# VectorE's order at three layer ends of a two-layer encoder: a norm pass, a low part and a weight split queued later

## The chip, the cores and the metric

The kernel runs on one core of one Trainium2 chip. The metric is the time on the device in microseconds (us) of one execution; a kernel's time is the median of its runs. Beside the timed runs there is one profiled execution, whose trace gives the start and duration of every instruction on the engines: PE (TensorE), DVE (VectorE), ACT (ScalarE), POOL (GpSimd) and SP (SyncE, which only issues transfers here).

## The reference

512 tokens of width 1024 go through two layers. Each layer has a token mixer and an MLP of width 4096, and each of these four is followed by a residual sum and a LayerNorm:

```python
def reference(x, ...):
    for i in range(DEPTH):                      # DEPTH = 2
        j = i // N_MIXERS
        if i % N_MIXERS == 0:
            m = _mixer_gdn(x, ...)              # gated delta rule, both directions, 8 heads of 128
        else:
            m = _mixer_gla(x, ...)              # gated linear attention, both directions, 4 heads
        x = _layernorm(DEEPNORM_ALPHA * x + m.astype(x.dtype), ln1_g[i], ln1_b[i])
        x = _layernorm(DEEPNORM_ALPHA * x + _sq_relu_mlp(x, mlp_w1[i], mlp_w2[i]).astype(x.dtype), ln2_g[i], ln2_b[i])
    return x
```

Both mixers end in a product of the mixed heads (512 x 1024) with `w_out` (1024 x 1024). The MLP is `relu(x w1)` squared, times `w2`. All is float32.

## The kernel before, in words

**Arithmetic.** Every large product is made of three matmuls on rounded halves: an operand is split into a high part, a cast on ScalarE, and a low part, a subtraction on VectorE (`split`, L96 and L101 for weights and hidden values). A product is high x high (L122), then the two mixed ones (L123, L124), made in `mm3`. Where a matmul is named `pj<-xth,wh`, `pj` is the PSUM bank it adds to, and `xth` / `xtl` are the high and low parts of the transposed activations, `wh` / `wl`, `ah` / `al`, `w2h` / `w2l` those of weight blocks or of other operands.

**Stages.** In the trace, the delta-rule mixer takes about the first 425 us, the first MLP runs from 425 to 762, the linear-attention mixer (`gla`) from 752 to 1004, the second MLP from 1004 to the end. The 512 tokens are four tiles of 128 (tile 0 to 3; `xt` 5559 to 5562 in the queues shown below). A layer's normed output is wanted transposed by the next layer's first products, which run in two halves of 256 tokens (tiles 0 and 1, then 2 and 3); the work of tiles 2 and 3 at a layer's end thus runs beside the first half of the next layer's products.

**A layer end** does for each tile:
- the last matmuls of the sublayer into PSUM, and the residual sum on VectorE (L332 at a mixer's end; L625, the line of `full`, at the MLP's, whose bank is `pX`); at the delta-rule mixer's end the residual is added on TensorE instead (`in_ps=True`);
- mean and variance. `layernorm` (the delta-rule mixer's end) uses VectorE's statistics, `norm_halves` (the others) adds up the mean on VectorE (L259), squares on ScalarE (L249, L250) and adds the variance (L264);
- a first norm pass of two halves, (z - mean) x gain (L236 or L263);
- the reciprocal root (`rsqrt`: L196 and L197 on ScalarE, then L198, L199, L200, L205 on VectorE, each of which needs the one before);
- a second pass of two halves, times that root, plus the bias (L241 or L270);
- `xpose`: two groups of four transposes on TensorE (L184) into a bank `tp`, a cast to `xth` on ScalarE (L187), a subtraction to `xtl` on VectorE (L188), for each group.

The `tp` banks are one at the delta-rule mixer's end and two in `gla`. After a mixer, VectorE adds high and low of the activations up again for a block scheme of the MLP (`x_blocks`, L420 and L426 to L429 into memory called `w2r`).

**Weights.** `wcols` loads a block of 128 columns (512 KB) into a staging buffer `wst` (three of them, by SyncE's queue, L50) and splits it. The first three blocks of the MLP's `w1` are loaded and split before its start (`take_ahead`); the fourth goes to memory called `ah` / `al`. SyncE's queue is in order: a load that waits for a free buffer holds those behind it, among them the loads of `w2` (`w2r`).

**The first work of `gla`** has a low-rank product `gps` (L147, L148) and, on ScalarE, the gate weights `w2r` (L847, L848 here), which take memory that the MLP's norm parameters `ln` had.

**What sets the order.** Each engine runs its own queue in order. The order of the queues is set when the program is built, by a scheduler that follows the place in the program: what is written first comes first unless it isn't ready in the scheduler's own reckoning. Two means bend this. `in_order(engine)` ties the instructions written inside it on an engine in the order of writing; TensorE's order is tied so in most stages. `issue_after(i)` keeps the instructions written inside it behind instruction `i` in the queue of `i`'s engine; it adds no wait on the chip. `normed` holds the ScalarE and VectorE instructions of the last norm's rsqrt and second pass (`normed[1]` is the latter), `last_hi` and `last_lo` those of the last `xpose`.

`out_last` makes the last matmuls of a mixer's output, the norm and `xpose`. `mlp`'s `last` does the same for the MLP's end and returns `norm`, which is called for tiles 2 and 3 behind it; after the first MLP, `xpose` for those tiles is called in `gla`, between the matmuls of its first products.

Of the kernel before, what the change touches and what calls it, by code (L numbers as in the profile page):

```python
# [17 lines left out]
P = 128  # L18
# [3 lines left out]
NT = S // P  # L22
# [6 lines left out]
class Ctx:  # L29
# [279 lines left out]
    def out_last(self, w, ks, lhs, z, tags, par, homes=None, xtags=("tp",), ahead=None, in_ps=True):  # L309

        nc = self.nc
        homes = iter(homes or ())
        ws = [{k: self.wrows(w, k * P, hf * 512, next(homes, None)) for k in ks[hf][::2]} for hf in range(2)]
        if ahead:
            ahead()
        if not in_ps:
            sums = [self.small.tile([P, 2], F32, name="lns", tag="lns") for t in range(NT)]
            stats = [[self.small.tile([P, 2], F32, name=f"lnv{q}", tag=f"lnv{q}") for q in range(2)] for t in range(NT)]  # L320
        pss = {}
        for t, hf in [(t, hf) for t in range(NT - 2) for hf in range(2)] + [(NT - 2, 0), (NT - 1, 0), (NT - 2, 1), (NT - 1, 1)]:
            sl = slice(t * P, (t + 1) * P)
            ps = pss[t, hf] = self.bank([P, 512], F32, name="ob", tag=tags[hf % len(tags)])
            if in_ps:
                nc.tensor.matmul(ps, self.ident, z[t][hf], start=True, stop=False)
            for i, k in enumerate(ks[hf]):
                ah, al = lhs(k, sl)
                wh, wl = ws[hf][k - i % 2]
                self.mm3(ps, ah, al, wh[:, i % 2, :], wl[:, i % 2, :], not in_ps and i == 0, i == len(ks[hf]) - 1)  # L330
            if not in_ps:
                nc.vector.scalar_tensor_tensor(z[t][hf], ps, 1.0, z[t][hf], ALU.mult, ALU.add, accum_out=sums[t][:, hf:hf + 1])  # L332
                self.half_stats(z[t][hf], sums[t][:, hf:hf + 1], stats[t][hf], ps)
            if hf:
                if in_ps:
                    self.layernorm([pss[t, 0], pss[t, 1]], self.xh(t), par)
                else:
                    self.norm_halves(z[t], par, sums[t], stats[t], (0, 1))
                if in_ps or t < NT - 2:
                    self.xpose(t, self.xt[t], xtags)  # L340
        if not in_ps:
            with self.tc.issue_after(self.normed[1].ins):
                self.xpose(NT - 2, self.xt[NT - 2], xtags)
            self.xpose(NT - 1, self.xt[NT - 1], xtags)


def mlp(c, w1, w2, g, b, out=None, extra=None):
# [8 lines left out]
    tc, nc = c.tc, c.nc  # L356
# [5 lines left out]
    with c.banks(pj=2, X=2, Y=2, Z=2), tc.tile_pool(name="mlp", bufs=2) as pool:  # L362
# [5 lines left out]
        def ring(name):  # L368
            return (pool, *RING[name])
# [36 lines left out]
        def new_h():  # L406
            return [pool.tile([P, HF, S], F32, name="h", tag="h", bufs=3) for _ in range(2)]
# [192 lines left out]
        def last(gi, h, a):  # L600
# [90 lines left out]
            for j in range(2):  # L691
# [1 line left out]
            return norm, second_normed  # L693

        h = new_h()
        specs = [(c.ahead[f] if f < len(c.ahead) else c.wcols(w1, f * P, pool=ring("ah") if f == 3 else None),
                  "pj", ("pj", "pj", "X", "X")[f]) for f in range(4)]
        for f, ps in enumerate(c.proj_halves(specs)):
            act(ps, h[0][:, f, :])
# [70 lines left out]
            h, a = nh, stream.a  # L770
        with c.in_order(mybir.EngineType.PE):
            norm, normed = last(G - 1, h, a)
        norm(2)
        norm(3)
        c.normed = normed

# [123 lines left out]
class GlaHead:  # L900
# [199 lines left out]
    def norm(self):  # L1100

        c, h = self.c, self.h
        V, A, T = c.nc.vector, c.nc.scalar, c.nc.tensor
        gcol = self.consts[-1]
        rs = c.small.tile([P, NT], F32, name="rs", tag="rs")
        c.rsqrt(rs, self.ss, NT, RMS_EPS)
        for n, o in self.ob.items():
            V.scalar_tensor_tensor(o, o, rs[:, n:n + 1], self.sr[:, n, :], ALU.mult, ALU.mult)
        for i in range(2):
            ps = c.bank([P, NT, P], F32, name="otp", tag="tp")  # L1110
            for n in range(NT):
                T.transpose(ps[:, n, :], self.ob[n][:, i * P:(i + 1) * P], c.ident)
            hi = self.oth[:, 2 * h + i, :].rearrange("p (n t) -> p n t", n=NT)
            lo = self.otl[:, 2 * h + i, :].rearrange("p (n t) -> p n t", n=NT)
            A.mul(hi, ps, gcol[:, i:i + 1])
            V.scalar_tensor_tensor(lo, ps, gcol[:, i:i + 1], hi.bitcast(F32), ALU.mult, ALU.subtract)
# [654 lines left out]
def body(tc, nc, a, out):  # L1771
    with contextlib.ExitStack() as es:
        def pool(name, bufs, **kw):
            return es.enter_context(tc.tile_pool(name=name, bufs=bufs, **kw))

        c = Ctx(tc, nc, (pool("const", 1), pool("big", 1), pool("wst", 3), pool("whl", 3), pool("small", 4)))
        x = a["x"][0]
        gdn(c, a["a_w_in"][0], a["a_conv"][0], a["a_alog"][0], a["a_dt_bias"][0], a["a_norm_g"][0],
            a["a_w_out"][0], a["ln1_g"][0], a["ln1_b"][0], x, a["mlp_w1"][0])
        with tc.tile_pool(name="gcst", bufs=1) as gp:  # L1780
            gc = []
            mlp(c, a["mlp_w1"][0], a["mlp_w2"][0], a["ln2_g"][0], a["ln2_b"][0],
                extra=lambda tmp: gc.append(GlaConst(c, gp, a["b_gate_b"][0], a["b_norm_g"][0], tmp)))
            gla(c, gc[0], a["b_w_in"][0], a["b_gate_w2"][0], a["b_w_out"][0], a["ln1_g"][1], a["ln1_b"][1], a["mlp_w1"][1])
        mlp(c, a["mlp_w1"][1], a["mlp_w2"][1], a["ln2_g"][1], a["ln2_b"][1], out=out[0])
# [18 lines left out]
```

## Time and profile before

| what | value |
|---|---|
| median of 3 runs | 1340.41 us (1339.39 to 1340.73) |
| profiled execution | 1341.23 us, of which the span from the first to the last instruction 1339.4 |
| mean granted TensorE clock | 0.996 |
| busy: PE / DVE / ACT / POOL | 1317.2 / 1099.9 / 800.5 / 123.3 us |
| read from HBM / written | 113.99 MB / 2.10 MB |

TensorE has work in nearly the whole span; the clock that it was granted is full but for the first and last slices. A row of the timeline has the start, the duration, the engine, the line, the operation, the tiles (out<-in), the shape and how many alike (x2) are put together, and in brackets for how long the engine stood idle before it and what it waited for. Small differences in idle time on TensorE show in the distance from one start to the next, too. Rows of "waits" give an engine, an operation and line, whom it waited for, the us in all, how often, and the longest.

### The profile page before, as it was taken

Reading aid. Unit: us, or ns where it says so; the run is one execution under the profiler, and the core shown is the slowest. Engines: PE = TensorE matmul, PEld = TensorE weight load, DVE = VectorE, ACT = ScalarE, POOL = GpSimd, SP = SyncE. Lnnn points to the kernel's source line nnn. Section 1 sums busy time; section 2 is a strip of 40 time slices with the busy share of each in tenths; the row PEclk is TensorE's granted clock in tenths of the full one; section 3 lists DMA queues with packets and bytes.
Section 4 is the critical chain, followed back from the end, with each engine's and each line's share of the span. In section 5 each row is a group of like instructions: output and inputs, shape, how many; then the busy total and the mean of one; then the engine's idle time right before and its main releaser. Section 6 shows DMA issues by size and latency. Waiting matters only on the chain.

```text
span 1339.4 us, 22232 instructions
## 1 busy us (share of the span) xinstructions
PE 1317.2 (98%) x8629; PEld 1124.4 (84%) x8629; DVE 1099.9 (82%) x1802; ACT 800.5 (60%) x1590; POOL 123.3 (9%) x177
## 2 busy tenths in 40 slices
PE   8999999999999999999999999999999999999996
PEld 8777878777777889999998888888889899999985
DVE  6797878788778878988988877967879678989888
ACT  4667657767643645666566754654456456565656
POOL 4000000000000910100102100000001001101011
PEclk9999999999999999999999999999999999999998
DMA  6221112112232674775748532221327475757556
GB/s 179 64 65 47 35 46 64 48 49 72 72 96 63 210 161 149 161 179 150 171 124 176 138 111 71 63 64 63 94 64 208 107 186 137 165 170 147 156 136 148
DMA packets 155660, 154.35 MB, mean 115 GB/s; under 512 B 7723, under 2 KB 122531, under 8 KB 155555
## 3 DMA queue, kind: packets, MB, share of 16 engines
q1 hardware_dynamic: 143779, 110.85, 27.8%
q0 software_dynamic: 11776, 42.08, 16.1%
q8 instruction: 68, 1.11, 0.3%
q14 instruction: 37, 0.30, 0.1%
HBM read 113.99 MB, written 2.10 MB: 87 GB/s over the span
## 4 chain that ended last, share of the span: by engine, by line
PE 86%; DVE 6%; ACT 6%; issue 1%; DMA 1%; DVEq 0%; POOL 0%; ACTq 0%; POOLq 0%
PE pX L123 3%; PE pX L122 3%; PE pX L124 3%; PE fx L124 3%; PE fx L123 3%; PE fx L122 3%; PE pjv L123 3%; PE m L1694 3%; PE pjv L122 3%; PE pjv L124 3%; PE pj L123 3%; PE pj L124 3%; PE pj L122 3%; PE fyz L124 2%; PE fyz L122 2%; PE fyz L123 2%
## 5 line engine op out<-in xcount | busy, mean ns | idle before, releaser
L101 DVE TENSOR_TENSOR wl<-wst,wh 128x1024 fp32r<-128x1024 f32 x148 | 182.3, 1232 | 49.1 <-ACT wh L96 47.8
L96 ACT CAST wh<-wst 128x1024 fp32r<-128x1024 f32 x150 | 157.7, 1051 | 101.1 <-PE fyz L123 30.1
L101 DVE TENSOR_TENSOR w2l<-w2r,w2h 128x1024 fp32r<-128x1024 f32 x92 | 112.7, 1225 | 27.2 <-ACT w2h L96 27.1
L96 ACT CAST w2h<-w2r 128x1024 fp32r<-128x1024 f32 x94 | 98.4, 1048 | 56.3 <-PE pX L124 24.8
L402 POOL DMA_DIRECT2D w2r<-w2r x56 | 48.4, 891 | 503.1 <-DVE w2l L101 290.1
L96 ACT CAST ah<-h 128x1024 fp32r<-128x1024 f32 x56 | 58.8, 1051 | 51.8 <-PE pZ L123 23.2
L451 DVE TENSOR_TENSOR wst<-wst 128x512 f32<-128x512 f32 x110 | 73.5, 688 | 0.2
L101 DVE TENSOR_TENSOR al<-h,ah 128x1024 fp32r<-128x1024 f32 x56 | 68.6, 1224 | 5.2 <-ACT ah L96 5.2
L123 PE MATMUL pX<-w2l,ah 128*128 128x512 f32 x168 | 66.1, 394 | 0.0
L122 PE MATMUL pX<-w2h,ah 128*128 128x512 f32 x168 | 66.0, 393 | 0.0
L124 PE MATMUL pX<-w2h,al 128*128 128x512 f32 x168 | 65.7, 391 | 0.0
L123 PE MATMUL pj<-xtl,wh 128*128 128x256 f32 (+1 forms) x192 | 64.6, 338 | 0.6 <-DVE xtl L188 0.6
L122 PE MATMUL pj<-xth,wh 128*128 128x256 f32 (+1 forms) x192 | 64.2, 338 | 0.3 <-ACT xth L187 0.2
L124 PE MATMUL pj<-xth,wl 128*128 128x256 f32 (+1 forms) x192 | 64.5, 337 | 0.0
L122 PE MATMUL pjv<-wh,xth 128*128 128x512 f32 x128 | 54.4, 425 | 0.0
L124 PE MATMUL pjv<-wh,xtl 128*128 128x512 f32 x128 | 50.2, 392 | 0.0
L123 PE MATMUL pjv<-wl,xth 128*128 128x512 f32 x128 | 50.0, 390 | 0.0
L124 PE MATMUL fx<-xh,wl 128*128 128x256 f32 x176 | 49.7, 283 | 0.0
L124 PE MATMUL fyz<-xh,wl 128*128 128x256 f32 x176 | 49.7, 282 | 0.0
L124 PE MATMUL fx<-xth,wl 128*128 128x256 f32 x176 | 49.7, 282 | 0.0
L123 PE MATMUL fx<-xtl,wh 128*128 128x256 f32 x176 | 49.7, 282 | 0.0
L122 PE MATMUL fyz<-xh,wh 128*128 128x256 f32 x176 | 49.7, 282 | 0.0
(528 smaller groups left out, 4319.1 us busy)
## 6 DMA issues: line engine op xcount, KB each, us to landing
wst<-in_mlp_w SPq DMA_DIRECT2D x68, 512.0 KB, 4.9
w2r<-in_mlp_w SPq DMA_DIRECT2D x60, 512.0 KB, 4.4
w2r<-w2r POOLq DMA_DIRECT2D x56, 512.0 KB, 5.6
wst<-in_a_w_in SPq DMA_DIRECT2D x32, 512.0 KB, 4.0
wst<-in_b_w_in SPq DMA_DIRECT2D x32, 256.0 KB, 3.0
wst<-in_a_w_out SPq DMA_DIRECT2D x8, 512.0 KB, 3.6
wst<-in_b_w_in SPq DMA_DIRECT2D x8, 512.0 KB, 4.2
wst<-in_b_w_out SPq DMA_DIRECT2D x8, 512.0 KB, 3.7
```

The costliest lines, as they stand in the source:

```text
L96: h = nc.scalar.copy(hi, src)
L101: self.halves = h, nc.vector.tensor_tensor(lo, src, hi.bitcast(F32), ALU.subtract)
L122: mm(ps, ah, bh, start=start, stop=False, **kw)
L123: mm(ps, ah, bl, start=False, stop=False, **kw)
L124: self.last_mm = mm(ps, al, bh, start=False, stop=stop, **kw)
L402: nc.gpsimd.dma_start(blocks[a + (q,)], blocks[b + (q,)], accum_op=ALU.add)
L451: plus = lambda a, b: V.tensor_tensor(a, a, b, ALU.add)
L1694: T.matmul(ps[:, d, :], *ops(d), start=True, stop=True)
```

## The change

Three edits, all on the order in which work is queued; no instruction is added or taken away.

1. `out_last`: the `xpose` calls of tiles 2 and 3 come behind the whole loop at the delta-rule mixer's end too (`in_ps=True`), with the lows of tile 2 behind tile 3's second norm pass. Before, this held for `gla`'s end alone.
2. `mlp`: in the second MLP (`out` is given) the split of the fourth weight block gets a place behind the last `xpose`'s high and low.
3. `mlp`: after the first MLP, `norm(2)` gets a place behind tile 1's second norm pass.

```diff
--- before.py
+++ after.py
@@ -336,12 +336,11 @@
                     self.layernorm([pss[t, 0], pss[t, 1]], self.xh(t), par)
                 else:
                     self.norm_halves(z[t], par, sums[t], stats[t], (0, 1))
-                if in_ps or t < NT - 2:
+                if t < NT - 2:
                     self.xpose(t, self.xt[t], xtags)
-        if not in_ps:
-            with self.tc.issue_after(self.normed[1].ins):
-                self.xpose(NT - 2, self.xt[NT - 2], xtags)
-            self.xpose(NT - 1, self.xt[NT - 1], xtags)
+        with self.tc.issue_after(self.normed[1].ins):
+            self.xpose(NT - 2, self.xt[NT - 2], xtags)
+        self.xpose(NT - 1, self.xt[NT - 1], xtags)
 
 
 def mlp(c, w1, w2, g, b, out=None, extra=None):
@@ -693,7 +692,8 @@
             return norm, second_normed
 
         h = new_h()
-        specs = [(c.ahead[f] if f < len(c.ahead) else c.wcols(w1, f * P, pool=ring("ah") if f == 3 else None),
+        specs = [(c.ahead[f] if f < len(c.ahead) else c.wcols(w1, f * P, pool=ring("ah") if f == 3 else None,
+                                                                 late=() if out is None else (c.last_hi, c.last_lo)),
                   "pj", ("pj", "pj", "X", "X")[f]) for f in range(4)]
         for f, ps in enumerate(c.proj_halves(specs)):
             act(ps, h[0][:, f, :])
@@ -770,7 +770,8 @@
             h, a = nh, stream.a
         with c.in_order(mybir.EngineType.PE):
             norm, normed = last(G - 1, h, a)
-        norm(2)
+        with contextlib.nullcontext() if out is not None else tc.issue_after(normed[1].ins):
+            norm(2)
         norm(3)
         c.normed = normed
```

From the first edit on, the new program's lines are one lower (L625 is L624, L420 is L419), and behind the third one higher (L847 is L848). How the queues stand:

VectorE at the end of the delta-rule mixer, before; `xt_5562` is tile 3, the L188 are lows of tiles 2 and 3, `al<-wst,ah` is the fourth weight block's low, and `w2r<-xth,xtl` the first sums of `x_blocks`:

```order
L205 TENSOR_TENSOR rstd<-rsy,rst 128x1
L241 SCALAR_TENSOR_TENSOR xt_5562<-xt_5562,rstd,lnp 128x512
L188 TENSOR_TENSOR xtl<-tp,xth 128x4x128
L241 SCALAR_TENSOR_TENSOR xt_5562<-xt_5562,rstd,lnp 128x512
L188 TENSOR_TENSOR xtl<-tp,xth 128x4x128
L101 TENSOR_TENSOR al<-wst,ah 128x1024
L188 TENSOR_TENSOR xtl<-tp,xth 128x4x128 x2
L420 TENSOR_TENSOR w2r<-xth,xtl 128x1024 x4
```

Tile 2's first low stands between the halves of tile 3's second pass, its second low ahead of `al`. The same place in VectorE's queue now:

```order
L205 TENSOR_TENSOR rstd<-rsy,rst 128x1
L241 SCALAR_TENSOR_TENSOR xt_5562<-xt_5562,rstd,lnp 128x512 x2
L188 TENSOR_TENSOR xtl<-tp,xth 128x4x128
L101 TENSOR_TENSOR al<-wst,ah 128x1024
L188 TENSOR_TENSOR xtl<-tp,xth 128x4x128 x3
L419 TENSOR_TENSOR w2r<-xth,xtl 128x1024 x3
L101 TENSOR_TENSOR wl<-wst,wh 128x1024
L419 TENSOR_TENSOR w2r<-xth,xtl 128x1024
```

Tile 3's second pass (L241) is no longer parted by tile 2's first low, tile 2's second low goes behind `al`, and a weight block's low (`wl`) goes ahead of the last of the four sums. On ScalarE, the cast to `ah` goes ahead of the cast of tile 2's second group. On TensorE, tile 2's second group of transposes and tile 3's stand later among the MLP's first matmuls.

VectorE at the end of the first MLP, before; `xt_5560` is tile 1, `xt_5561` tile 2, `xt_5562` tile 3, the first of the L188 are lows of tiles 0 and 1:

```order
L198 TENSOR_TENSOR rst<-rsy 128x1
L625 SCALAR_TENSOR_TENSOR xt_5561,lns<-pX,xt_5561 128x512
L199 SCALAR_TENSOR_TENSOR rst<-bmv,rst 128x1
L259 SCALAR_TENSOR_TENSOR bmv<-lns,bias_83 128x1
L200 TENSOR_SCALAR rst<-rst 128x1
L263 SCALAR_TENSOR_TENSOR xt_5561<-xt_5561,bmv,ln 128x512
L205 TENSOR_TENSOR rstd<-rsy,rst 128x1
L188 TENSOR_TENSOR xtl<-tp,xth 128x4x128
L270 SCALAR_TENSOR_TENSOR xt_5560<-xt_5560,rstd,ln 128x512 x2
L188 TENSOR_TENSOR xtl<-tp,xth 128x4x128 x3
L263 SCALAR_TENSOR_TENSOR xt_5561<-xt_5561,bmv,ln 128x512
L625 SCALAR_TENSOR_TENSOR xt_5562,lns<-pX,xt_5562 128x512
```

Tile 2's mean and first pass stand on both sides of tile 1's second pass. The same place in VectorE's queue now:

```order
L198 TENSOR_TENSOR rst<-rsy 128x1
L624 SCALAR_TENSOR_TENSOR xt_5561,lns<-pX,xt_5561 128x512
L199 SCALAR_TENSOR_TENSOR rst<-bmv,rst 128x1
L200 TENSOR_SCALAR rst<-rst 128x1
L205 TENSOR_TENSOR rstd<-rsy,rst 128x1
L270 SCALAR_TENSOR_TENSOR xt_5560<-xt_5560,rstd,ln 128x512 x2
L188 TENSOR_TENSOR xtl<-tp,xth 128x4x128 x4
L624 SCALAR_TENSOR_TENSOR xt_5562,lns<-pX,xt_5562 128x512
L259 SCALAR_TENSOR_TENSOR bmv<-lns,bias_83 128x1
L264 SCALAR_TENSOR_TENSOR bmv<-lnv_8590,lnv_8591,lnt 128x1
L263 SCALAR_TENSOR_TENSOR xt_5561<-xt_5561,bmv,ln 128x512 x2
```

Tile 2's mean (L259) and its first pass (both L263) stood ahead of and behind tile 1's second pass and now stand behind tile 3's residual sum (L624). The four steps of tile 1's root follow each other with only tile 2's residual sum between them. TensorE's, ScalarE's and the other queues are as before here.

VectorE at the end of `gla`, before; `xt_5562` is tile 3, the first L188 row has tile 2's lows, the second tile 3's:

```order
L270 SCALAR_TENSOR_TENSOR xt_5562<-xt_5562,rstd,ln_9212 128x512
L270 SCALAR_TENSOR_TENSOR xt_5562<-xt_5562,rstd,ln_9214 128x512
L188 TENSOR_TENSOR xtl<-tp,xth 128x4x128 x2
L101 TENSOR_TENSOR al<-wst,ah 128x1024
L188 TENSOR_TENSOR xtl<-tp,xth 128x4x128 x2
L420 TENSOR_TENSOR w2r<-xth,xtl 128x1024 x4
```

The block's low stands between the lows of the two tiles. The same place in VectorE's queue now:

```order
L270 SCALAR_TENSOR_TENSOR xt_5562<-xt_5562,rstd,ln_9212 128x512
L270 SCALAR_TENSOR_TENSOR xt_5562<-xt_5562,rstd,ln_9214 128x512
L188 TENSOR_TENSOR xtl<-tp,xth 128x4x128 x4
L419 TENSOR_TENSOR w2r<-xth,xtl 128x1024
L101 TENSOR_TENSOR al<-wst,ah 128x1024
L419 TENSOR_TENSOR w2r<-xth,xtl 128x1024 x3
```

The fourth block's low (`al`) stood between the lows of tiles 2 and 3 and now stands behind all of them and the first sum of `x_blocks`. On ScalarE the cast to `ah` goes behind both casts of tile 3. SyncE's queue has the same rows here: the load that needs `al`'s staging buffer stands ahead of two loads of `w2r`.

## The prediction

> **What bounds the kernel now.** I read the page's busy times first, then TensorE's list of waits over the whole run, then the core's span and clock, and then the three layer ends in the timeline, engine by engine.
>
> ```profile
> PE 1317.2 (98%) x8629; PEld 1124.4 (84%) x8629; DVE 1099.9 (82%) x1802; ACT 800.5 (60%) x1590; POOL 123.3 (9%) x177
> PE tp L184 <- DVE xt L270: 1.5, 3, 1.0
> PE pj L123 <- DVE xtl L188: 0.6, 1, 0.6
> PE gps L148 <- DVE xtl L188: 0.3, 1, 0.3
> PE pj L122 <- ACT xth L187: 0.2, 1, 0.2
> core 0: 1339.4 us, clock 0.996
> ```
>
> TensorE is busy in 98% of the span, at a granted clock of 0.996. The change touches no matmul, so it can only gain where TensorE stands still. The four waits above (us in all, times, longest) are those at the three layer ends that it touches, 2.6 us together: whatever the reordering does for VectorE's 1099.9 us, it can win little more than 0.2% of the span.
>
> The sum is made on the profiled run: 1341.23 us with a span of 1339.4, 0.82 above the median of 1340.41. A gain of so many us in the span is taken off the median. A measurement of this kernel can tell about 0.2%, 2.7 us, from no change; the three runs shown spread over 1.3 us.
>
> **Place A, the end of the delta-rule mixer (about 430 to 440 us).** The rows of before, first VectorE, then ScalarE, then TensorE:
>
> ```profile
> 432.55 0.68 DVE L188 TENSOR_TENSOR xtl<-tp,xth 128x512 fp32r<-128x512 f32 x1
> 433.15 0.74 DVE L241 SCALAR_TENSOR_TENSOR xt<-xt,rstd,lnp 128x512 f32<-128x512 f32 x1
> 434.70 0.69 DVE L188 TENSOR_TENSOR xtl<-tp,xth 128x512 fp32r<-128x512 f32 x1 [0.80 <-ACT xth L187]
> 435.70 1.41 DVE L101 TENSOR_TENSOR al<-wst,ah 128x1024 fp32r<-128x1024 f32 x1 [0.31 <-POOL tmp L787]
> 434.56 1.05 ACT L96 CAST ah<-wst 128x1024 fp32r<-128x1024 f32 x1
> 435.44 0.66 PE L184 MATMUL tp<-ident,xt 128*128 128x128 f32 x4
> 436.28 0.28 PE L123 MATMUL pj<-xtl,ah 128*128 128x256 f32 x1
> 436.78 0.51 PE L122 MATMUL pj<-xth,wh 128*128 128x256 f32 x2 [0.21 <-ACT xth L187]
> 437.17 0.38 PE L124 MATMUL pj<-xth,al 128*128 128x256 f32 x1
> ```
>
> Now L241 of tile 3 runs as a pair, so tile 2's first low starts 0.6 later (432.55 to about 433.2) and the fourth block's `ah` can start when the pair ends, at about 433.35 instead of 434.56. `al` follows at about 434.5, ahead of tile 2's second low, which then runs at about 435.8 to 436.5 (before: 434.70). There is one PSUM bank for these transposes, so tile 3's first group must wait for that low; in TensorE's new order it stands later, and I put TensorE there at about 436.67. The matmuls of 128x256 go 0.12 apart. Before, 436.28 to 436.78 held 0.38 more than one step, and the pair at 436.78 another 0.15: some 0.5 of standing still. After, I find at most 0.1 at the first use of `al` (ready 435.87, TensorE there about then). Term A: -0.4. Its bounds are -0.6, if the slow transposes at 435.44 (0.65 to the next matmul, 0.36 elsewhere) go too, and +0.7, if the held low comes as late as the second rival below has it. VectorE's x-block sums come later by a microsecond at most, and what hides that is TensorE's stock of work: its list of waits from 436 to 737 us holds nothing but the 0.2 above.
>
> **Place B, the end of the first MLP (745 to 763 us).** VectorE, then TensorE, then ScalarE:
>
> ```profile
> 746.88 0.16 DVE L198 TENSOR_TENSOR rst<-rsy 128x1 f32<-128x1 f32 x1
> 746.95 0.69 DVE L625 SCALAR_TENSOR_TENSOR xt<-pX,xt 128x512 f32<-128x512 f32 x1
> 747.94 0.75 DVE L263 SCALAR_TENSOR_TENSOR xt<-xt,bmv,ln 128x512 f32<-128x512 f32 x1
> 749.28 1.40 DVE L270 SCALAR_TENSOR_TENSOR xt<-xt,rstd,ln 128x512 f32<-128x512 f32 x2
> 756.61 1.41 DVE L270 SCALAR_TENSOR_TENSOR xt<-xt,rstd,ln 128x512 f32<-128x512 f32 x2
> 757.94 0.15 DVE L198 TENSOR_TENSOR rst<-rsy 128x1 f32<-128x1 f32 x1
> 758.12 0.16 DVE L199 SCALAR_TENSOR_TENSOR rst<-bmv,rst 128x1 f32<-128x1 f32 x1
> 758.70 1.42 DVE L270 SCALAR_TENSOR_TENSOR xt<-xt,rstd,ln 128x512 f32<-128x512 f32 x2
> 762.10 1.29 DVE L188 TENSOR_TENSOR xtl<-tp,xth 128x512 fp32r<-128x512 f32 x2 [0.79 <-ACT xth L187]
> 748.67 0.40 PE L124 MATMUL pX<-h,al 128*128 128x512 f32 x1
> 750.07 1.32 PE L184 MATMUL tp<-ident,xt 128*128 128x128 f32 x8 [1.00 <-DVE xt L270]
> 757.50 1.23 PE L184 MATMUL tp<-ident,xt 128*128 128x128 f32 x8
> 762.31 0.28 PE L147 MATMUL gps<-xth,wh 128*64 128x256 f32 x1
> 762.85 0.34 PE L148 MATMUL gps<-xtl,wh 128*64 128x256 f32 x1 [0.26 <-DVE xtl L188]
> 760.20 0.62 ACT L847 CAST w2r<-w2f 64x512 fp32r<-64x512 f32 x1 [0.84 <-DVE xt L270]
> 760.83 0.63 ACT L848 ACTIVATE w2r<-w2f 32x512 fp32r<-32x512 f32 x1
> 761.48 1.07 ACT L187 CAST xth<-tp 128x512 fp32r<-128x512 f32 x2
> ```
>
> Before, tile 2's mean (L259) and a first pass (L263 at 747.94) stand ahead of tile 1's second pass, and TensorE waits for that pass until 750.07; at a step of 0.23 it would have been there at 748.90. After, L198, L625, L199, L200, L205 take 746.88 to 748.13, three of them 0.19 apart since each needs the one before (757.94 to 758.12 shows that step). Tile 1's pass starts at 748.13, 1.15 earlier, and the wait of 1.0 is gone.
>
> But the two first passes are not gone, they are queued behind tile 3's L625. From there: the pass of tile 1 to 749.46, four lows at 0.61 to 751.91, L625 to 752.52, two small ones to 752.78, tile 2's L263 pair (2 x 0.67) to 754.11, then tile 3's two L263 with six small ones between them, which so hide most of tile 2's rstd chain, to 756.1. So tile 2's second pass starts at 756.1 instead of 756.61, and tile 3's, with a bare chain of three steps before it, at 758.03 instead of 758.70. TensorE, 1.15 early, waits for tile 2 about 0.8 and keeps 0.5. The end of the place is the chain tile 3's L270, ScalarE's L847 and L848 (the `w2r` memory comes free with tile 3's last pass), the high, the low, L148: it moves with L270, from 762.85 to about 762.18. Term B: -0.67. Bounds: -0.9, where TensorE's own arrival at L148 ends it (the 0.5 it keeps, and 0.42 for which it stands between 762.31 and 762.85 beyond one step), and -0.2, if the L263 pairs run as slowly as some rows of this form do (0.75 rather than 0.67 each, four of them, and the small steps 0.19 apart).
>
> The Trainium skill, "VectorE: DVE Perf Modes", section "The DRAIN you can't avoid", says that a semaphore between two VectorE instructions costs nothing beyond the pipe's emptying. The rows disagree for these small ones: dependent they go 0.18 to 0.20 apart, independent ones 0.07 (746.88 to 746.95). By the page tile 3's bare chain would be 0.36 shorter, B would end at its bound of -0.9, and the sum below at -1.6.
>
> **Place C, the end of the second mixer (1010 to 1014 us).** VectorE, ScalarE, TensorE, then SyncE's queue and, from the DMA view of 1004 to 1036 us, the us to landing:
>
> ```profile
> 1011.49 1.23 DVE L101 TENSOR_TENSOR al<-wst,ah 128x1024 fp32r<-128x1024 f32 x1
> 1012.63 1.28 DVE L188 TENSOR_TENSOR xtl<-tp,xth 128x512 fp32r<-128x512 f32 x2
> 1011.67 1.19 ACT L187 CAST xth<-tp 128x512 fp32r<-128x512 f32 x2 [0.22 <-PE tp L184]
> 1028.35 1.05 ACT L96 CAST wh<-wst 128x1024 fp32r<-128x1024 f32 x1
> 1013.37 0.39 PE L123 MATMUL pj<-xtl,wh 128*128 128x256 f32 x1 [0.56 <-DVE xtl L188]
> 1012.74 0.37 SPq L50 DMA_DIRECT2D wst<-in_mlp_w  x1
> wst<-in_mlp_w SPq DMA_DIRECT2D x4, 512.0 KB, 6.3
> ```
>
> `al` no longer stands ahead of tile 3's lows. That frees 1.14 on VectorE, but the low also needs the high, which ends at about 1011.67 + 0.59 = 1012.26 and waited for the transposes, not for `ah`. So the low starts at 1012.29 instead of 1012.63 and L123 at 1013.03 instead of 1013.37. Term C: -0.34, with 0.1 and 0.4 as bounds (an `al` still partly in the way, the high a little sooner). `ah` then runs at about 1012.9 to 1013.9 and `al`, behind one x-block sum, at 1014.8 to 1016.0. TensorE first uses the block at 1017.07 (the row below), so a microsecond hides it. The next weight load waits for `al` (it frees the staging slot), and goes at about 1016.1 instead of 1012.74, with two loads of `w2r` behind it on SyncE's queue.
>
> ```profile
> 1017.07 0.28 PE L122 MATMUL pj<-xth,ah 128*128 128x256 f32 x1
> ```
>
> **Sum.** -0.4 - 0.67 - 0.34 = -1.4: 1339.8 for a profiled run, 1339.0 for the median. The bounds of the three terms give -1.9 to +0.4.
>
> **The rivals.** First, *more*: every term at its good end, -0.6 - 0.9 - 0.4 = -1.9, 1338.5. For it speaks that before loses more between issues than the listed waits say; against it that B then needs tile 3's chain faster than the rows show.
>
> Second, *A gives it back*: `ah` does not start earlier than before (434.56), because it waits for something that these rows do not separate (434.56 is where a high left ScalarE free, so before shows only that `ah` was ready by then). Then `al` runs at 435.7 and the low queued behind it at 437.04 to 437.72, where before it was done at 435.39. Tile 3's transposes start at 437.8, 1.1 behind TensorE's arrival: A is +0.7, B and C stay, and the sum is -0.3, 1340.1. It decides once `ah` is later than about 433.5. Against it: `ah` waits for tile 3's last L241, and that is 0.6 earlier.
>
> Third, *slower, by SyncE's queue at C*: the three loads go 3.3 us later. The staged block is cast at 1028.35; landing at 1016.1 + 6.3 = 1022.4 it has 5.9 to spare, so it decides only if the load takes over 12 us, twice the median shown. If the whole 3.3 came through, the sum would be -1.4 + 3.3 = +1.9, 1342.3.
>
> That the change does nothing is no rival: the queues differ as described; that its gains vanish is the second.
>
> **The numbers.** The forecast of -1.4 has a chance of 0.56, *more* 0.15, *A gives it back* 0.20, the queue 0.09. The range: downward everything that TensorE stands still at the three places, counted between issues, is 0.5 + 0.3 at A, 1.2 + 0.4 at B and the listed 0.6 at C, 3.0 together, so 1337.4; upward the +0.4 of the bounds with half the spread of the three runs (0.7), so 1341.5. The queue is left out. All cases lie within 2.7 us of before as worked out; only their scatter leads beyond it: most of *more* and some of the forecast with a gain I have missed, 0.11; two thirds of the queue, if its price is larger than one delay, 0.06; same 0.83.
>
> **What would show it.** Right: TensorE's wait for tile 1's L270 (1.0) is gone and a wait for tile 2's of 0.5 to 0.9 stands in its place; L148 comes about 1.1 earlier in the span (A and B together); L123's wait falls from 0.56 to about 0.2; `ah` starts before the high of tile 2's second half at A. Wrong: a new wait at the first `al`, at tile 3's transposes, or at a `wh` between 1020 and 1036 us; or any difference over 0.3 us in a stretch between the three places.

## The result, and the profile after

The changed kernel takes 1338.49 us (median of 20 runs, 1337.02 to 1339.36) beside 1340.51 (20 runs, 1338.59 to 1341.17) for the kernel before: a ratio of 0.9987, 95% interval 0.9982 to 0.9993. That is 2.0 us faster, with 0.9 to 2.4 in the interval; the forecast was 1.4. The runs of each kernel lie in two groups (before 8 runs up to 1339.43 and 12 from 1340.29; after 9 up to 1337.76, at a granted clock of 0.997 or 0.998, and 11 from 1338.36, at 0.996), and the medians inside the groups differ by 1.5 and 1.6 us, so some tenths of the 2.0 are the luck of where the middle run fell. The profiled run's span is 1337.1 us (before 1339.4).

TensorE's list of waits of after, the lines that answer to those of before:

```profile
PE tp L184 <- DVE xt L270: 1.1, 3, 0.6
PE pj L123 <- DVE xtl L188: 0.2, 1, 0.2
```

The wait of 1.0 for tile 1's second pass is gone and one of 0.6 for tile 2's has come; L123's fell from 0.6 to 0.2; the waits of L148 and of the first `xth` at place A are no longer listed.

Where the time went is read by setting TensorE's 8629 matmuls of two traces side by side, the first with the first, and so on, and taking the difference of their starts, each counted from its trace's first matmul. The change of that difference across a stretch (in us of before's span) is what the stretch won or lost:

| kernel against before | 0-60 | 60-423 | A 423-445 | 445-737 | B 737-765 | 765-1000 | C 1000-1020 | 1020-end |
|---|---|---|---|---|---|---|---|---|
| after | -0.60 | -0.12 | -0.63 | -0.01 | -0.79 | +0.11 | -0.35 | +0.01 |
| edit 1 alone | -0.20 | +0.33 | -0.65 | -0.01 | 0.00 | -0.10 | -0.01 | 0.00 |
| edit 3 alone | -1.67 | +0.32 | +0.01 | -0.01 | -0.77 | +0.21 | -0.01 | +0.03 |
| edit 2 alone | -1.77 | +0.24 | +0.01 | -0.01 | 0.00 | -0.17 | -0.33 | 0.00 |
| `ah` behind | -1.97 | +0.11 | +0.56 | -0.01 | -0.77 | -0.01 | -0.33 | -0.01 |
| gate weights behind | -0.12 | +0.12 | -0.62 | 0.00 | -1.08 | +0.01 | -0.33 | -0.01 |
| `norm(2)` between | -0.47 | +0.30 | -0.63 | -0.01 | +0.15 | +0.08 | -0.33 | 0.00 |
| last low alone | -0.36 | +0.16 | -0.63 | 0.00 | -0.77 | +0.01 | -0.34 | 0.00 |

The three places give -1.77 in after, of -2.38 in all. The first 60 us hold the same instructions in the same order in all kernels and differ by up to 2 us: that column is not the change but the start of the one execution that was profiled (the last section). The stretches 60-423 and 765-1000, where the order is the same too, scatter by a few tenths.

**Place A in after**, VectorE, ScalarE, then TensorE:

```profile
431.16 1.42 DVE L241 SCALAR_TENSOR_TENSOR xt<-xt,rstd,lnp 128x512 f32<-128x512 f32 x2
432.49 0.68 DVE L188 TENSOR_TENSOR xtl<-tp,xth 128x512 fp32r<-128x512 f32 x1
433.75 1.23 DVE L101 TENSOR_TENSOR al<-wst,ah 128x1024 fp32r<-128x1024 f32 x1 [0.57 <-POOL tmp L786]
434.89 0.68 DVE L188 TENSOR_TENSOR xtl<-tp,xth 128x512 fp32r<-128x512 f32 x1
432.61 1.05 ACT L96 CAST ah<-wst 128x1024 fp32r<-128x1024 f32 x1 [1.15 <-DVE xt L241]
433.43 0.60 PE L184 MATMUL tp<-ident,xt 128*128 128x128 f32 x4
433.79 0.36 PE L124 MATMUL pj<-xth,wl 128*128 128x256 f32 x1
435.02 0.38 PE L124 MATMUL pj<-xth,al 128*128 128x256 f32 x1
435.84 0.60 PE L184 MATMUL tp<-ident,xt 128*128 128x128 f32 x4
436.20 0.36 PE L124 MATMUL pj<-xth,al 128*128 128x256 f32 x1
437.84 0.66 PE L184 MATMUL tp<-ident,xt 128*128 128x128 f32 x4
438.25 0.36 PE L122 MATMUL pj<-xth,ah 128*128 128x256 f32 x1
```

`ah` starts as soon as the undivided pass ends, `al` ends at 434.98, and TensorE takes it at 435.02, 0.08 later than its step of 0.12 would have it (the matmul before starts at 434.82). Tile 3's first transposes (435.84) follow without a stop, and the next matmul stands 0.36 behind; in before it stood 0.65 behind.

**Place B in after**, VectorE, TensorE, ScalarE:

```profile
746.38 0.15 DVE L200 TENSOR_SCALAR rst<-rst 128x1 f32<-128x1 f32 x1
746.56 0.16 DVE L205 TENSOR_TENSOR rstd<-rsy,rst 128x1 f32<-128x1 f32 x1
746.76 1.42 DVE L270 SCALAR_TENSOR_TENSOR xt<-xt,rstd,ln 128x512 f32<-128x512 f32 x2
754.65 1.42 DVE L270 SCALAR_TENSOR_TENSOR xt<-xt,rstd,ln 128x512 f32<-128x512 f32 x2
756.55 1.41 DVE L270 SCALAR_TENSOR_TENSOR xt<-xt,rstd,ln 128x512 f32<-128x512 f32 x2
747.57 1.32 PE L184 MATMUL tp<-ident,xt 128*128 128x128 f32 x8
755.55 1.23 PE L184 MATMUL tp<-ident,xt 128*128 128x128 f32 x8 [0.57 <-DVE xt L270]
760.69 0.33 PE L148 MATMUL gps<-xtl,wh 128*64 128x256 f32 x1
758.04 0.62 ACT L848 CAST w2r<-w2f 64x512 fp32r<-64x512 f32 x1 [0.64 <-DVE xt L270]
```

Set against before, matmul by matmul, TensorE gains 1.14 at tile 1's transposes (747.57), gives back 0.55 at tile 2's (755.55, with its new wait) and gains 0.19 at L148 (760.69).

**Place C in after**, VectorE, ScalarE, TensorE, SyncE:

```profile
1010.25 1.29 DVE L188 TENSOR_TENSOR xtl<-tp,xth 128x512 fp32r<-128x512 f32 x2 [0.77 <-ACT xth L187]
1012.59 1.22 DVE L101 TENSOR_TENSOR al<-wst,ah 128x1024 fp32r<-128x1024 f32 x1
1009.63 1.19 ACT L187 CAST xth<-tp 128x512 fp32r<-128x512 f32 x2 [2.03 <-PE tp L184]
1010.99 0.39 PE L123 MATMUL pj<-xtl,wh 128*128 128x256 f32 x1 [0.22 <-DVE xtl L188]
1013.83 0.37 SPq L50 DMA_DIRECT2D wst<-in_mlp_w  x1
```

VectorE now stands idle 0.77 in front of tile 3's lows, since the high is what comes last. The weight load behind `al` is issued 2.84 us after L123; in before it went 0.63 ahead of it.

### The profile page after: what moved, and what is told of

It is laid out like the page before. It is cut to its first block, busy times and chain, and to the rows that moved or that the text cites. A ratio compares the mean times of both kernels' runs of the same rounds, so it can differ in the third digit from the quotient of the medians.

```text
span 1337.1 us, 22233 instructions
## 1 busy us (share of the span) xinstructions
PE 1315.7 (98%) x8629; PEld 1123.4 (84%) x8629; DVE 1098.5 (82%) x1802; ACT 800.1 (60%) x1590; POOL 124.2 (9%) x177
## 4 chain that ended last, share of the span: by engine, by line
PE 87%; DVE 6%; ACT 5%; issue 1%; DMA 1%; DVEq 0%; POOL 0%; ACTq 0%; POOLq 0%
PE pX L123 3%; PE pX L122 3%; PE pX L124 3%; PE fx L124 3%; PE fx L123 3%; PE fx L122 3%; PE pjv L123 3%; PE m L1695 3%; PE pjv L122 3%; PE pjv L124 3%; PE pj L123 3%; PE pj L124 3%; PE pj L122 3%; PE fyz L124 2%; PE fyz L122 2%; PE fyz L123 2%
## 5 line engine op out<-in xcount | busy, mean ns | idle before, releaser
L123 PE MATMUL pX<-w2l,ah 128*128 128x512 f32 x168 | 66.1, 394 | 0.0
L123 PE MATMUL pj<-xtl,wh 128*128 128x256 f32 (+1 forms) x192 | 64.7, 338 | 0.2 <-DVE xtl L188 0.2
L123 PE MATMUL pjv<-wl,xth 128*128 128x512 f32 x128 | 50.0, 391 | 0.0
L123 PE MATMUL fx<-xtl,wh 128*128 128x256 f32 x176 | 49.7, 282 | 0.0
```

Source lines behind the costliest of these rows:

```text
L123: mm(ps, ah, bl, start=False, stop=False, **kw)
```

## The experiments

**The three edits apart.** Each is before with one edit of the diff.

Edit 1 alone:

> Before with edit 1 alone. If the three gains are separate and add up, TensorE's matmuls, set side by side with those of before one by one, gain 0.74 us between 430 and 440 us as in the trace of after, and nothing behind that (within 0.2); the median falls by 0.7, ratio about 0.9995. If the gain of 2.0 in the median owes to something else (the start of the run, or an edit that helps through the next place), A's part is under 0.3 or the later places move too.

Edit 3 alone:

> Before with edit 3 alone. Separate gains: 1.05 us earlier at tile 1's transposes, 0.56 of it given back at tile 2's, 0.21 won at the last L148, in all 0.70 between 745 and 763 us, none elsewhere; ratio about 0.9995. If the later place of VectorE's first passes only moves the wait, the sum is within 0.2 of nothing.

Edit 2 alone:

> Before with edit 2 alone. Separate gains: 0.37 us at the first L123 of the second half (1010 to 1014 us), nothing before and nothing after it; ratio about 0.9997. If SyncE's later weight load came through, a step of up to 3.3 us the other way would stand between 1020 and 1040 us.

Measured: 1339.06 us (11 runs), ratio 0.9994 (0.9986 to 1.0003); 1339.91 (11), 0.9995 (0.9986 to 1.0004); 1340.12 (11), 0.9999 (0.9991 to 1.0008), beside 1340.53 for before. No interval excludes 1: the times cannot tell the single edits from nothing. The table can: each edit moves its own place, within 0.02 of the amount that it has in after (-0.65, -0.77, -0.33), and neither of the other two. They are separate and add up to -1.75. (The 0.74 and 0.70 that the expectations name for A and B in after are not the table's, which has 0.63 and 0.79.) No step the other way follows edit 2 between 1020 us and the end, so the third rival's queue is refuted, as far as this delay goes.

**What A's gain needs.** The split of the fourth block is kept behind tile 2's second high:

```diff
             self.xpose(NT - 2, self.xt[NT - 2], xtags)
+        self.mid_hi = self.last_hi
...
-                  late=() if out is None else (c.last_hi, c.last_lo)),
+                  late=(c.mid_hi,) if out is None else (c.last_hi, c.last_lo)),
```

> After, with the fourth block's split at A kept behind the cast of tile 2's second group, so that tile 3's norm pass stays a pair but the cast to ah does not run ahead. If A's gain is the early ah and TensorE's order that follows from it, tile 3's first transposes wait about 0.7 for tile 2's second low, the six semaphore steps behind them cost their 0.3 again, the first use of al waits 0.3, and A is 0.4 to 0.5 us slower than before (1.2 slower than after). If the undivided norm pass is what gains, A stays at -0.7.

Measured: A +0.56 against before (1339.86 us, 10 runs, ratio 0.9998, 0.9989 to 1.0007). TensorE in this kernel:

```profile
434.30 0.66 PE L184 MATMUL tp<-ident,xt 128*128 128x128 f32 x4 [0.57 <-DVE xtl L188]
434.95 0.36 PE L122 MATMUL pj<-xth,ah 128*128 128x256 f32 x1
435.63 0.62 PE L122 MATMUL pj<-xth,wh 128*128 128x256 f32 x3 [0.21 <-ACT xth L187]
```

Edit 1 without the early `ah` is a loss: tile 3's first transposes wait 0.57 for the low, the next matmul comes 0.65 behind them again, and a wait for the next high follows. (That third wait was for `xth`, as in before, not for `al`.) A's gain is the early `ah` and the order of TensorE's queue that comes with it; this run does not tell the two apart. This is also the second rival made to happen; it had +0.7.

**What ends place B.** The gate weights' casts go behind tile 3's highs:

```diff
-            nc.scalar.copy(w2r[d][0:64, :], w2f[0:64, d, :])
-            nc.scalar.mul(w2r[d][R[2], :], w2f[R[2], d, :], -1.0)
+            with tc.issue_after(c.last_hi.ins):
+                nc.scalar.copy(w2r[d][0:64, :], w2f[0:64, d, :])
+                nc.scalar.mul(w2r[d][R[2], :], w2f[R[2], d, :], -1.0)
```

> After, with the four ScalarE casts of the gate weights (L848, L849) queued behind tile 3's highs instead of between tile 2's and tile 3's. If the end of B is set by the chain tile 3's second pass, L848, L849, high, low, L148, the high starts when its transposes are done, about 0.7 earlier, L148 no longer waits, and B is 0.4 us better than after: -1.2 against before instead of -0.78, and the median about 0.4 below after's. If TensorE's arrival or VectorE sets it, B stays at -0.78. If the gate weights now come late, a wait of up to 1.3 us stands at their first matmul (lg, 768 us in after).

Measured: B -1.08, 0.29 better than after (0.4 was expected); 1338.87 us (11 runs), ratio to before 0.9989 (0.9980 to 0.9998). ScalarE, then TensorE:

```profile
759.43 1.08 ACT L187 CAST xth<-tp 128x512 fp32r<-128x512 f32 x2 [1.27 <-PE tp L184]
761.09 0.28 PE L147 MATMUL gps<-xth,wh 128*64 128x256 f32 x1
761.20 0.28 PE L148 MATMUL gps<-xtl,wh 128*64 128x256 f32 x1
```

The high now waits for its transposes alone and L148 follows L147 at its own step, so the chain over L848 and L849 did set the end of B in after, and TensorE's arrival sets it here. No wait at the gate weights' first matmul appears. By the trace this is the best of the versions; by the times it cannot be told from after (the intervals overlap).

**Whether the order at B only moves the wait.** Tile 2's first pass goes ahead of tile 3's residual sum:

```diff
             for j in range(2):
                 full(2 + j, 0, X[j])
+                if j == 0 and out is None:
+                    with tc.issue_after(second_normed[1].ins):
+                        norm(2)
...
-        with contextlib.nullcontext() if out is not None else tc.issue_after(normed[1].ins):
+        if out is not None:
             norm(2)
```

> After, with tile 2's mean and first pass ahead of tile 3's residual sum instead of behind it, still behind tile 1's second pass. If VectorE's work from there to tile 3's second pass is one fixed amount and the order only moves the wait, tile 2's second pass comes 0.9 earlier and the wait of 0.57 at its transposes is gone, tile 3's second pass comes about 1.5 later and a wait of 1.3 to 1.5 stands at tile 3's transposes, and B ends within 0.3 of after's -0.78. If the wait for tile 2 was the loss itself, B gains about 0.5 more, -1.3.

Measured: B +0.15 in a single run (1340.22 us), which neither theory had. VectorE, then TensorE:

```profile
756.78 1.29 DVE L188 TENSOR_TENSOR xtl<-tp,xth 128x512 fp32r<-128x512 f32 x2
758.75 1.41 DVE L270 SCALAR_TENSOR_TENSOR xt<-xt,rstd,ln 128x512 f32<-128x512 f32 x2
755.44 1.23 PE L184 MATMUL tp<-ident,xt 128*128 128x128 f32 x8
759.55 1.32 PE L184 MATMUL tp<-ident,xt 128*128 128x128 f32 x8 [1.46 <-DVE xt L270]
762.25 0.28 PE L148 MATMUL gps<-xtl,wh 128*64 128x256 f32 x1
```

The wait for tile 2 is gone and one of 1.46 for tile 3 has come, as expected. What I had wrong is what follows: I let L148 end at the time of its chain, but behind a late transposition TensorE still has its own 2.7 us of work up to L148, and that now sets the time. In this order tile 2's two lows (756.78) also go ahead of tile 3's rstd chain, which stands bare again. So the order does not only move the wait; each order has its own sum. This single run has no interval, and it moved the lows as well as the pass, so it does not price the pass alone.

**What gains at C.** The fourth block's split in the second MLP is held behind the last low alone, so that on ScalarE its cast goes ahead of tile 3's highs, as in before:

```diff
-                  late=() if out is None else (c.last_hi, c.last_lo)),
+                  late=() if out is None else (c.last_lo,)),
```

> After, with the fourth block's split in the second MLP held behind the last low alone: on ScalarE the cast to ah stands ahead of tile 3's highs again as in before, on VectorE al stays behind the lows. If al's place on VectorE is what gains at C, C stays at -0.33 to -0.35. If the cast's place on ScalarE is, C falls to -0.1 or less.

Measured: C -0.34, in a single run (1339.29 us). VectorE, then TensorE:

```profile
1010.70 1.29 DVE L188 TENSOR_TENSOR xtl<-tp,xth 128x512 fp32r<-128x512 f32 x2 [0.77 <-ACT xth L187]
1011.90 1.22 DVE L101 TENSOR_TENSOR al<-wst,ah 128x1024 fp32r<-128x1024 f32 x1
1011.44 0.39 PE L123 MATMUL pj<-xtl,wh 128*128 128x256 f32 x1 [0.23 <-DVE xtl L188]
```

With the cast ahead of the highs VectorE still stands idle 0.77 for the high and L123 waits 0.23, as in after: the place of `al` on VectorE is the whole of it.

## Why the prediction was right

**Direction and size.** The sum was -1.4; the three places measure -1.75 to -1.77, the median -2.0 with the sum inside its interval. The mechanism at each place is the forecast's, but the size lies between the forecast and the first rival, *more* (-1.9), and nearer to the latter: A came out beyond the rival's bound of -0.6, B about half way to its -0.9, C as forecast. None of the signs of being wrong came: no new wait at `al`, at tile 3's transposes or behind 1020 us, and -0.01 and +0.11 between the places. L148 came 1.42 earlier by A and B together, for about 1.1 forecast.

**Term C, -0.34:** -0.33 to -0.35 in six traces. The step that carried it, that the high comes next after `al` is out of the way, is seen as VectorE's 0.77 of waiting for `xth`. The slack of a microsecond at `al` held.

**Term B, -0.67:** -0.77 to -0.79. The parts: tile 1's wait gone for 1.14 (forecast 1.15), given back at tile 2 0.55 (0.65), and the end set by tile 3's pass and the ScalarE casts, which the experiment showed. The sum of VectorE's queue held to 0.1: tile 2's pass comes 7.89 us behind tile 1's (754.65 less 746.76; forecast 756.1 less 748.13, 7.97) and tile 3's 9.79 (forecast 9.90), which is the 0.1 that B is over. The bound of -0.9 was too near: with TensorE's own arrival as the end (the gate weights behind), B is -1.08. The Trainium skill, "VectorE: DVE Perf Modes", section "The DRAIN you can't avoid", as the prediction read it, would have had B at -0.9; the dependent steps still stand 0.18 to 0.20 apart in after (746.38, 746.56, 746.76), and B ended short of it. That reading went too far: these steps last 0.15 and 0.16 us, so each starts 0.03 to 0.04 behind the end of the one before, and the section's measurement, which is of copies, is not contradicted. The 0.07 set against it in the prediction is between instructions that do not need each other.

**Term A, -0.4:** -0.62 to -0.65, the mis-sized one. The wait of 0.38 and the 0.15 went as forecast, and the first `al` cost 0.08. What I had only as the bound is the slow transposes of before: 0.65 to the next matmul, 0.29 more than the usual 0.36. With 0.09 lost at tile 3's second group (it starts 0.04 late, and the next matmul stands 0.41 behind it), 0.38 + 0.15 + 0.29 - 0.08 - 0.09 gives the 0.65. The trace shows six semaphore steps of TensorE's own queue there, 0.11 apart, ahead of the first matmul with `ah`. Each waits for two semaphores of transfers, of which the latest had landed at 413.28. The page and the timeline leave such steps out; the trace's own records have them, here in before (us, length in us, line):

```
435.45 0.051 L122 EVENT_SEMAPHORE
435.56 0.051 L122 EVENT_SEMAPHORE
435.66 0.051 L122 EVENT_SEMAPHORE
435.77 0.051 L122 EVENT_SEMAPHORE
435.88 0.051 L122 EVENT_SEMAPHORE
435.98 0.051 L122 EVENT_SEMAPHORE
```

In before they came right behind a wait (435.45 to 435.98), when the queue had no work in stock, and the weight load of that matmul starts at 436.06, right behind the last of them, though `ah` was done at 435.61; in after they lie at 433.30 to 433.83, behind queued matmuls, and the transposes there take the usual 0.36 (433.43 to 433.79). The same six follow the wait in the kernel with `ah` behind, and the 0.65 is back. The late group without such steps is the one of 0.41 in after (437.84 to 438.25). So by these traces about 0.25 of A is whether the steps are hidden; no run took them away by themselves.

**The rivals.** *A gives it back* didn't happen, but its mechanism is real: with `ah` late, A loses 0.56. *More* had its condition fulfilled at A, where before did lose more between issues than the listed waits say, and not at B. The load at C came 3.1 us later against the matmuls ahead of the place (forecast 3.3), and nobody waited for it.

**The range and the chances.** The median lies in the range. At 1338.49 it falls on the 1338.5 of *more*, which is partly luck: by the three places alone the time would be 1338.7. The 0.2% given as what can be told from no change was too wide: 20 runs tell 0.13% from no change here, and -2.0 us is inside what the text called "same".

## What to carry to other kernels

An instruction's place in a queue is worth what the last releaser behind it allows: take the blocker out, and the next one (here the high at C, tile 2's pass at B) bounds the gain: at C it was 0.35 for an `al` of 1.23. Work it out by writing the queue's instructions one after another with durations from neighbouring rows, small dependent ones with their gaps, and let TensorE's own work behind a late step count as well as the chain. For changes of a microsecond in a thousand, set the matmuls of two traces side by side; in a short stretch around the edit the difference repeats here within 0.03 us, where 20 timed runs of each leave an interval of 1.5.

## What was not expected

**The start of a run is worth up to 2 us, whatever the kernel.** The windows view of the first 20 us of before, and then of edit 2 alone; the columns are span, busy time of PE, PEld (TensorE's weight loads), DVE, ACT and POOL, granted clock, DMA share and GB/s:

```profile
0.00:20.00 20.00, 16.53 (x104) 15.89 (x105) 10.95 (x25) 8.33 (x15) 5.28 (x23) 0.91 0.79 227
```

```profile
0.00:20.00 20.00, 16.67 (x119) 16.16 (x120) 11.31 (x26) 9.71 (x16) 5.27 (x23) 1.00 0.85 246
```

The same instructions are granted 0.91 of the clock in one execution and 1.00 in the other, and TensorE gets through 119 matmuls instead of 104. Six of the nine profiles have the 0.91, after among them; the three without it are those with -1.67 to -1.97 in the table's first column.

The trace's own records of the granted clock tell more. The clock first rises to full between 5.0 and 7.5 us (at 7.15 in before: the transposes there start 0.21 us apart until then and 0.11 from then on; the windows view counts that first stretch as 1.00). In the six profiles it falls to half 3.41 us behind the rise and stays there for 3.41 us, which costs about half of that, 1.7 us (edits 2 and 3 alone, without it, have -1.77 and -1.67 in the table's first column). Between rise and fall, TensorE waits 1.9 to 2.1 us for VectorE (L165); in the three profiles without the fall it waits there for 1.8, 1.8 and, with the earliest rise (5.01), 2.1 us.

The Trainium skill, "TensorE: Matmul & The Clock Gate", section "Part 1: The HAM clock gate (the "warmup" mystery)", has half speed after an idle window of about 3.4 us; the length of the half-speed stretch agrees, but TensorE's idle time ahead of it is shorter here than that window. The same section has the window run free of the kernel's start, which would let the same program meet it in one execution and not in the next, and would fit a rise that moves by 2.5 us. No run here was made for that, and the cause stays open.

**A satisfied wait can cost TensorE time.** The six semaphore steps at A, 0.11 us apart, cost nothing while the queue runs ahead of the array, and the traces put about 0.25 us on them behind a stall.
